# Attention's v turns in one copy and one difference each, filling products over both sequence halves of one w_o tile, the second w_o tile split behind them

## The chip, the cores and the metric

The kernel runs on one core of a Trainium2 chip. Its time is the time on the device of one execution, in microseconds (us); the median of several runs counts. The profile comes from one more execution, recorded by the hardware profiler. Engines are named as in the profile: PE multiplies matrices, PEld loads its weights, DVE works on vectors, ACT computes functions and copies, POOL is a third engine for elementwise work, and SP issues the transfers (DMAs). Each engine works through its own queue in order and waits there for the others by semaphores.

## The reference

Two layers of a decoder work on a sequence of 1024 positions of width 1024, in 32-bit floats. Layer 0 mixes with a linear recurrence, layer 1 with stick-breaking attention of 16 heads of 64 columns; a SwiGLU network follows each. What matters here is the attention:

```
qkv = einsum("bsd,de->bse", x, w_qkv)            # x: normalized input of the layer
for each block of 128 queries, keys s < t only:
    z        = q @ k.T / sqrt(64)
    log_fail = log_sigmoid(-z)                   # 0 where s >= t
    suffix   = reverse_cumsum(log_fail) - log_fail
    weights  = exp(log_sigmoid(z) + suffix)      # 0 where s >= t
    out      = weights @ v
o = concatenate(outs)                            # all heads side by side
return einsum("bse,ed->bsd", o, w_o)             # then h = h + this
```

## The kernel before

**Numbers in two parts.** Each 32-bit operand of a matrix product is split into a rounded high part and a low remainder. A product is then three matmuls, high by high, high by low, low by high (`mm3`, L141 to L143). A split is a copy on ACT (the high part) and a difference on DVE (the low part).

**Layout.** Activations lie transposed: 8 tiles of 128 columns of the model by 1024 positions, in two halves `n` of 512 positions. `xh[k][n]` and `xl[k][n]` are the parts of column tile k, half n. They hold the attention's input first, and take its result afterwards. In the profile they are called vh, vl and xg, after the memory that they share.

**The attention** goes through 8 pairs `q` of heads. A generator `fill` (`all_fill`) gives the projections of q, k and v for the next pair (`qkv_steps`), one `mm3` at a time, to be put between the steps of the present pair, which leave PE waiting otherwise. The loop at the end of `trunk` runs over units `u`, each a block of 128 keys against 512 queries. In one step of it stand, in this order: the scores of a later chunk (`z_part`, two matmuls into z_ps), the transposes of the weights of unit u + 2 (`t_part`, into wt_ps) and their split (`t_split`: ACT copy th at L1474, DVE difference tl at L1475), the rest of the chunk (`z_rest`), one deferred task from the list `later`, two steps of `fill`, and the products of unit u with v (`av_part`, L1486 and L1487, into av_ps).

`z_rest` makes two sigmoids on ACT (L1445, L1446), a scan on DVE from the right end of the chunk (L1449, L1451) and a product on POOL (L1452). F has one column more than the chunk, for what stands to its right. In chunks on the diagonal POOL sets it to 0 (L1438); for the four off-diagonal chunks of a head it is copied from `sofar[j]`, one column of 128, by ACT (L1441). POOL writes `sofar[j]` (L1454).

**A turn of v.** v must lie with the positions on the partitions, so each half of each pair's v is transposed in four blocks into a PSUM bank (`v_turn`, L1401). The bank holds 4 blocks by 2 heads by 64 columns. For each head in turn, ACT copies its 256 columns to the high part (L1405) and DVE forms the low part (L1406). The turns use the two buffers of the projections, but for the last one (pair 7, half 1), which borrows one of the two buffers of the weights' transposes, with tag "T".

**The end of the attention.** When all projections are done, `all_fill` goes on with products of the output projection: it splits the second tile of w_o (`mix[0].proc(1)`, ACT L168 and DVE L169), takes a PSUM tile `ob` with two halves, and multiplies, for the first two tiles of w_o in the order 0, 4, 1, 5, ..., half 0 of the column tiles k = 0 to 6, one `mm3` in every other step. Column tile 7 is missing, since the last pair of heads still computes it. Results of earlier pairs went to DRAM and are brought back by `bring_back` (L1315, L1316), both halves in one go.

Column tile 7 of half n is ready once `gather` (ACT L1496, DVE L1497) has put the two heads together and `parts` (ACT L1502, DVE L1503) has split them; for half 1 these are the last works of the attention.

`mix_out_ffn_in` follows. For its first four outputs it goes through (d, n) = (0, 0), (4, 0), (0, 1), (4, 1): the first two finish the halves of `ob` with column tile 7 of half 0, the third and fourth start in fresh banks (`dense_in`, 24 matmuls each, ob_ps).

The order on each engine is written out by hand in these places (`manual_schedule`). Where two such blocks meet, the instructions of both mix, each block's own order kept: so the six matmuls that finish the halves of `ob` stand among the attention's last products.

Of the kernel before, what the change touches and what calls it, by code (L numbers as in the profile page):

```python
# [16 lines left out]
P = 128  # L17
S = 1024
D = 1024
ND = D // P  # L20
NT = S // P
NB = 512
NH = S // NB
# [3 lines left out]
HD = 64  # L27
# [6 lines left out]
def trunk(  # L34
# [22 lines left out]
    nc = tc.nc  # L57
    f32 = lambda t: t.bitcast(F32)
# [40 lines left out]
    xh, xl = [None] * ND, [None] * ND  # L99
# [40 lines left out]
    def mm3(ps, wh, wl, mh, ml, first, last, **kw):  # L140
        nc.tensor.matmul(ps, lhsT=wh, rhs=mh, start=first, stop=False, **kw)  # L141
        nc.tensor.matmul(ps, lhsT=wh, rhs=ml, start=False, stop=False, **kw)  # L142
        nc.tensor.matmul(ps, lhsT=wl, rhs=mh, start=False, stop=last, **kw)  # L143
# [98 lines left out]
    half = lambda t, n: t[:, n * NB : (n + 1) * NB]  # L242
# [119 lines left out]
    with ExitStack() as st:  # L362
# [152 lines left out]
        with tc.manual_schedule(engines={E.PE}):  # L515
            for what in "A0 A1 B0 A2 G0 A3 Y0 B1 Y1 A4 G1 A5 B2 Y2 A6 G2 A7 B3 Y3 B4 Y4 G3 B5 Y5 B6 Y6".split():
                {"A": stage_a, "B": stage_b, "G": stage_g, "Y": stage_y}[what[0]](int(what[1]))
            mix = last_tile(ND - 1)
# [78 lines left out]
    def mix_out_ffn_in(h, mix, bias, layer, gnext, ob):  # L597
# [3 lines left out]
        half = lambda t, i: t[:, i * NB : (i + 1) * NB]  # L601
# [8 lines left out]
        begun = ob is not None  # L610
        if begun:
            ps_.enter_context(pos)
        else:
            po = ps_.enter_context(tc.tile_pool(name="fpo", bufs=1, space=PSUM, reuse_waits="tile"))
            ob = po.tile([P, S], F32, name="ob")
# [106 lines left out]
        with tc.manual_schedule(engines={E.PE, E.Activation, E.DVE, E.Pool}):  # L722
# [11 lines left out]
            w = None  # L734
            for j in range(HK):
                rows = (j, j + HK)
                dn = [(d, n) for d in rows for n in range(NH)] if j else [(d, n) for n in range(NH) for d in rows]
                for k, (d, n) in enumerate(dn):
                    o = HK * j + k
                    if begun and o < 2:  # L740
                        ps = half(ob, o)
                        for i in range(2 if o == 0 else 0):
                            hi, lo = mix.w[rows[i]]
                            mm3(half(ob, i), hi[:, ND - 1], lo[:, ND - 1], xh[ND - 1][0], xl[ND - 1][0], False, True)
                    else:
                        ps = pp.tile([P, NB], F32, tag="p", name="ob_ps")
                        dense_in(ps, mix.w[d], n)
                    if bias is None:
                        V.tensor_add(h[d][n], ps, h[d][n])
                    else:  # L750
                        V.scalar_tensor_tensor(
                            h[d][n], ps, vc[:, bias + d : bias + d + 1], h[d][n], op0=ALU.add, op1=ALU.add
                        )
                    for i in loads.get(o, ()):
                        mix.load(i)
                    if o in procs:
                        mix.proc(procs[o])
                    if o == 10:
                        w = weights_in(0)
                    elif o == 11:  # L760
                        w.s12()
                        w.s2()
                        w.s3()
                        w.do_s4()
                    elif o == 12:
                        w.a_hi()
                        w.a_lo()
                    elif o == 14:
                        w.b_hi()
                        w.b_lo()  # L770
                        nw = weights_in(1)
                    if o < 15:
                        drain(2)
                    if sq_todo:
                        squares(h, *sq_todo.pop(0), rbc[1:], acc)
                if j == HK - 1:
                    xstk.close()
                    open_v(xstk, v, False)
                    rhs_in = {i: [v[i, j] for j in range(HK)] for i in range(NPROD)}
                todo.append(v_steps(h, v, j, gcol, ta, tb))  # L780
                sq_todo += [(d, n) for d in rows for n in range(NH)]
# [291 lines left out]
            for s_, (kind, x) in enumerate(steps):  # L1073
                w, nw, ahead = nw, nxt, None
# [218 lines left out]
    with ExitStack() as st:  # L1293
        ap = st.enter_context(tc.tile_pool(name="ap", bufs=1))
        qs, mix = ExitStack(), [Mix(w_o, 0)]
# [9 lines left out]
        Q, KK, VV = {}, {}, {}  # L1305
# [65 lines left out]
        def evacuate(q, which, n, ps):  # L1371
            full = lambda tag, m: [ap.tile([P, m, S], F32R, tag=tag, name=tag, bufs=4) for _ in range(2)]
            t = ap.tile([P, NB], F32, tag="t", name="t", bufs=2)
            nc.vector.tensor_mul(t, ps, rbc[n])
            yield
            cs = slice(n * NB, (n + 1) * NB)
            if which == 0 and n == 0:
                Q[q] = [t[:, 0] for t in full("q", 1)]
            if which == 1 and n == 0:
                KK[q] = full("kk", 2)  # L1380
            if which < 2:
                two = ap.tile([P, 2, NB], F32R, tag="two", name="two", bufs=2)
                nc.scalar.copy(two[:, 0], t)
                nc.vector.tensor_sub(two[:, 1], t, f32(two)[:, 0])
                for hx, (a, b) in enumerate(((top, bot), (bot, top))):
                    if which == 0:
                        nc.sync.dma_start(f32(Q[q][hx])[a, cs], f32(two)[a, 0])
                        nc.sync.dma_start(f32(Q[q][hx])[b, cs], f32(two)[a, 1])
                    else:
                        for half_ in (top, bot):  # L1390
                            nc.sync.dma_start(f32(KK[q][hx])[half_, :, cs], f32(two)[a])
                return
            if n == 0:
                VV[q] = ap.tile([P, NT, 2, P], F32R, tag="v", name="v", bufs=2)

            def v_turn():

                pool, tag = (psT, "T") if (q, n) == (NP - 1, 1) else (psQ, "qk")
                tp = pool.tile([P, NB], F32, tag=tag, name="vt_ps")
                for i in range(4):  # L1400
                    nc.tensor.transpose(tp[:, i * P : (i + 1) * P], t[:, i * P : (i + 1) * P], ident)  # L1401
                src = tp.rearrange("p (b h c) -> p b h c", b=4, h=2)
                bs = slice(4 * n, 4 * n + 4)
                for hx in range(2):
                    nc.scalar.copy(VV[q][:, bs, hx, 0:HD], src[:, :, hx])  # L1405
                    nc.vector.tensor_sub(VV[q][:, bs, hx, HD:P], src[:, :, hx], f32(VV[q])[:, bs, hx, 0:HD])  # L1406

            late.append(v_turn)
            if q == NP - 1 and n == 0:
                bring_back(*((p, 0) for p in range(NP - 2)))  # L1410
# [22 lines left out]
        def z_rest(ps, q, hx, j, ci, c0, c1, diag):  # L1433
            n = min(c1, (j + 1) * P) - c0
            F = ap.tile([P, NB + 32], F32, tag="F", name="F", bufs=4)
            first = 0.0
            if diag:
                nc.gpsimd.memset(F[:, n : n + 1], 0.0)  # L1438
            else:
                first = sofar[j]  # L1440
                nc.scalar.copy(F[:, n : n + 1], first)  # L1441
            tag = f"w{j}" if diag else "w"
            wt = ap.tile([P, n], F32, tag=tag, name=tag, bufs=1 if diag else 4)
            W[q, hx, j, ci] = wt
            nc.scalar.activation(F[:, 0:n], ps[:, 0:n], AF.Sigmoid, scale=-SC)  # L1445
            nc.scalar.activation(wt, ps[:, 0:n], AF.Sigmoid, scale=SC)  # L1446
            rev = F[:, 0:n][:, ::-1]
            if diag:
                nc.vector.tensor_tensor_scan(rev, rev, unit[:, NB - n :][:, ::-1], first, op0=ALU.mult, op1=ALU.add)  # L1449
            else:  # L1450
                nc.vector.tensor_tensor_scan(rev, rev, rev, first, op0=ALU.mult, op1=ALU.bypass)  # L1451
            nc.gpsimd.tensor_mul(wt, wt, F[:, 1 : n + 1])  # L1452
            if diag and j >= 4:
                nc.gpsimd.tensor_copy(sofar[j], F[:, 0:1])  # L1454
# [65 lines left out]
        def all_fill():  # L1520
            yield from first
            for q in range(1, NP):
                yield from qkv_steps(q)
            bring_back((NP - 2, 0), *((p, 1) for p in range(NP - 2)))
            yield
            yield
            late.pop()()
            qs.close()
            mix[0].proc(1)
            po = pos.enter_context(tc.tile_pool(name="fpo", bufs=1, space=PSUM, side="right", reuse_waits="tile"))  # L1530
            ob = po.tile([P, S], F32, name="ob")
            mix.append(ob)
            for i, d in enumerate(mix[0].order[:2]):
                w = mix[0].w[d]
                for k in range(ND - 1):
                    mm3(ob[:, i * NB : (i + 1) * NB], w[0][:, k], w[1][:, k], xh[k][0], xl[k][0], k == 0, False)
                    yield
                    yield

        fill = all_fill()  # L1540
        ready = {}
        E = mybir.EngineType
        with tc.manual_schedule(engines={E.PE, E.Activation, E.DVE, E.Pool, E.SP}):
# [3 lines left out]
            first = qkv_steps(0)  # L1547
# [16 lines left out]
            c = 0  # L1564
# [69 lines left out]
```

## Time and profile before

| | us |
|---|---|
| median of 3 runs | 2195.4 |
| lowest and highest run | 2195.05, 2197.01 |
| the profiled execution, its own time | 2195.37 |
| its span, from the first to the last instruction | 2193.6 |
| granted TensorE clock, mean over the span | 0.998 |

Rows of the profile read like this. In the busy times by stretch stand the stretch, its length, then for PE, PEld, DVE, ACT and POOL the busy time and the number of instructions, then the granted clock of TensorE (1.00 is full speed), the share of the DMA engines and GB/s. In groups of instructions stand line, engine, operation, output and inputs with their shapes and count, then busy time in us and the mean of one in ns, then the idle time of the engine before them and what ended it. In the order of time stand the start and the duration in us, and in brackets the idle time just before and who ended it. Waits have the engine and line that waited, who ended it, us in total, the number of times and the longest. In rows of one line of the code stand the least, the median and the greatest duration in ns. The duration of a matmul holds its way through the array: matmuls of 512 columns follow each other every 0.23 us, though each is shown with 0.39. Lines are those of the kernel before; in the changed kernel the attention's lines stand two later.

### The profile page before, as it was taken

The numbers are of one execution on the slowest core, as the hardware profiler recorded it, in microseconds if no ns is written. First come the engines' busy times: TensorE is split into PE (matmuls) and PEld (weight loads), VectorE is DVE, ScalarE is ACT, GpSimd is POOL, SyncE is SP. The second block draws the span as 40 slices with busy tenths as digits, with TensorE's granted clock in tenths as the row PEclk, the third lists the DMA queues.
The fourth block names the chain that finished last, engine by engine and source line by source line (L and its number), as shares of the span: only waits on it lengthen the run. The fifth ranks groups of instructions, "written<-read, shape, count | busy, mean of one in ns | idle before, by whom it ended". The sixth has DMA issues, their size and how long they took to land.

```text
span 2193.6 us, 28494 instructions
## 1 busy us (share of the span) xinstructions
PE 2167.9 (99%) x10120; PEld 1803.3 (82%) x10120; DVE 1711.4 (78%) x2383; ACT 1155.4 (53%) x2031; POOL 315.7 (14%) x443
## 2 busy tenths in 40 slices
PE   8999999999999999999999999999999999999998
PEld 6888888888888888888888888878888888888887
DVE  6887778667777887887888888876876777788886
ACT  5567435334444544556666666753543444454556
POOL 2222020000000000004444444531000000000002
PEclk9999999999999999999999999999999999999999
DMA  7111412334444764434333333551133444467442
GB/s 232 49 48 39 135 39 64 110 125 152 141 145 138 250 221 129 148 117 104 89 106 90 94 98 105 173 169 54 48 115 116 149 146 143 144 228 236 137 153 87
DMA packets 297677, 277.71 MB, mean 127 GB/s; under 512 B 15288, under 2 KB 214080, under 8 KB 297536
## 3 DMA queue, kind: packets, MB, share of 16 engines
q1 hardware_dynamic: 297520, 275.90, 40.6%
q8 instruction: 79, 1.29, 0.2%
q14 instruction: 62, 0.51, 0.1%
q10 hardware_dynamic: 16, 0.00, 0.0%
HBM read 175.71 MB, written 74.97 MB: 114 GB/s over the span
## 4 chain that ended last, share of the span: by engine, by line
PE 95%; DVE 2%; ACT 1%; DMA 1%; SPq 0%; issue 0%; DVEq 0%; ACTq 0%
PE p_ps L143 18%; PE p_ps L141 18%; PE p_ps L142 18%; PE qk_ps L143 4%; PE qk_ps L141 4%; PE qk_ps L142 4%; PE wt_ps L1465 3%; PE ob_ps L141 2%; PE ob_ps L142 2%; PE ob_ps L143 2%; PE a_ps L141 2%; PE a_ps L142 2%; PE a_ps L143 2%; PE z_ps L1427 2%; PE z_ps L1428 2%; PE av_ps L1487 2%
## 5 line engine op out<-in xcount | busy, mean ns | idle before, releaser
L1452 POOL TENSOR_TENSOR w<-w,F 128x128 f32<-128x128 f32 (+1 forms) x192 | 192.5, 1002 | 268.3 <-DVE F L1449 164.6
L141 PE MATMUL p_ps<-vh,wch 128*128 128x512 f32 x524 | 204.2, 390 | 0.0
L143 PE MATMUL p_ps<-vh,wal 128*128 128x512 f32 x524 | 204.1, 389 | 0.1
L143 PE MATMUL p_ps<-vh,wbl 128*128 128x512 f32 x524 | 204.1, 390 | 0.0
L143 PE MATMUL p_ps<-vh,wcl 128*128 128x512 f32 x524 | 204.1, 390 | 0.0
L141 PE MATMUL p_ps<-vh,wbh 128*128 128x512 f32 x524 | 204.1, 390 | 0.0
L142 PE MATMUL p_ps<-vl,wch 128*128 128x512 f32 x524 | 203.9, 389 | 0.0
L142 PE MATMUL p_ps<-vl,wbh 128*128 128x512 f32 x524 | 203.9, 389 | 0.0
L141 PE MATMUL p_ps<-vh,wah 128*128 128x512 f32 x524 | 203.9, 389 | 0.0
L142 PE MATMUL p_ps<-vl,wah 128*128 128x512 f32 x524 | 203.8, 389 | 0.0
L668 ACT CAST wbh<-sb 128x1024 fp32r<-128x1024 f32 (+2 forms) x69 | 69.6, 1009 | 193.1 <-DVE sb L652 193.1
L1474 ACT CAST th<-wt_ps 128x512 fp32r<-128x512 f32 x192 | 92.6, 482 | 126.3 <-PE wt_ps L1465 125.8
L212 POOL TENSOR_TENSOR acc<-acc,rbc 128x512 f32<-128x512 f32 x30 | 41.6, 1386 | 771.9 <-ACT rbc L211 771.9
L1475 DVE TENSOR_TENSOR tl<-wt_ps,th 128x512 fp32r<-128x512 f32 x192 | 105.6, 550 | 48.9 <-ACT th L1474 46.9
L141 PE MATMUL qk_ps<-vh,whi 128*128 128x512 f32 x264 | 118.1, 447 | 0.0
L1449 DVE TENSOR_TENSOR_SCAN F<-F,unit 128x128 f32<-128x128 f32 (+3 forms) x128 | 115.4, 902 | 2.8 <-ACT F L1445 2.6
L143 PEld LDWEIGHTS p_ps<-vh,wbl 128*128 128x128 f32 x524 | 98.4, 188 | 21.4 <-DVE wbl L672 0.8
L143 PEld LDWEIGHTS p_ps<-vh,wal 128*128 128x128 f32 x524 | 98.3, 188 | 21.4 <-DVE wal L663 1.0
L143 PEld LDWEIGHTS p_ps<-vh,wcl 128*128 128x128 f32 x524 | 98.3, 188 | 21.1 <-DVE wcl L682 0.6
L141 PEld LDWEIGHTS p_ps<-vh,wch 128*128 128x128 f32 x524 | 98.4, 188 | 20.8 <-ACT tb L1057 0.5
L141 PEld LDWEIGHTS p_ps<-vh,wah 128*128 128x128 f32 x524 | 98.4, 188 | 20.4
L142 PEld LDWEIGHTS p_ps<-vl,wah 128*128 128x128 f32 x524 | 98.4, 188 | 20.4
(341 smaller groups left out, 5858.3 us busy)
## 6 DMA issues: line engine op xcount, KB each, us to landing
raw<-in_ffn_w_in SPq DMA_DIRECT2D x88, 512.0 KB, 4.0
vl<-pd SPq DMA_DIRECT2D x128, 256.0 KB, 3.6
pd<-U SPq DMA_DIRECT2D x90, 256.0 KB, 2.3
kk<-two SPq DMA_DIRECT2D x64, 256.0 KB, 4.2
raw<-in_ffn_w_out SPq DMA_DIRECT2D x56, 256.0 KB, 3.9
raw<-in_attn_w_qkv SPq DMA_DIRECT2D x24, 512.0 KB, 4.1
raw<-in_lru_w_in SPq DMA_DIRECT2D x16, 512.0 KB, 4.0
q<-two SPq DMA_DIRECT2D x64, 128.0 KB, 2.3
```

Of the source, the lines that this page charges most:

```text
L141: nc.tensor.matmul(ps, lhsT=wh, rhs=mh, start=first, stop=False, **kw)
L142: nc.tensor.matmul(ps, lhsT=wh, rhs=ml, start=False, stop=False, **kw)
L143: nc.tensor.matmul(ps, lhsT=wl, rhs=mh, start=False, stop=last, **kw)
L668: nc.scalar.copy(self.full(self.wb), self.full(self.sb))
L1427: nc.tensor.matmul(ps[:, 0 : c1 - c0], lhsT=lhsT, rhs=KK[q][hx][:, 0, c0:c1], start=True, stop=False)
L1428: nc.tensor.matmul(ps[:, 0 : c1 - c0], lhsT=lhsT, rhs=KK[q][hx][:, 1, c0:c1], start=False, stop=True)
L1449: nc.vector.tensor_tensor_scan(rev, rev, unit[:, NB - n :][:, ::-1], first, op0=ALU.mult, op1=ALU.add)
L1452: nc.gpsimd.tensor_mul(wt, wt, F[:, 1 : n + 1])
L1465: nc.tensor.transpose(tp[:, c : c + P], W[q, hx, j, kb // 4][:, (kb % 4) * P : (kb % 4 + 1) * P], ident)
L1474: nc.scalar.copy(th[:, q0:], tp[:, q0:])
L1475: nc.vector.tensor_sub(tl[:, q0:], tp[:, q0:], f32(th)[:, q0:])
L1487: nc.tensor.matmul(ps[:, q0:], lhsT=VV[q][:, kb, hx], rhs=tl[:, q0:], start=False, stop=last)
```

## The change

- In `v_turn` the two copies become one over both heads, and the two differences one.
- In `z_rest` the one-column copy of `sofar[j]` into F goes from ACT to POOL.
- In `all_fill` the fourteen filling products take one tile of w_o, d = 0, with both halves, in place of tiles 0 and 4 with half 0. The split of the second w_o tile stands behind these products in place of ahead of them.
- In `mix_out_ffn_in` the first four outputs of the second layer are now (0, 0), (0, 1), (4, 0), (4, 1). Both halves of `ob` are finished at the start with column tile 7, each with its own half of it.

```diff
@@ mix_out_ffn_in
-                dn = [(d, n) for d in rows for n in range(NH)] if j else [(d, n) for n in range(NH) for d in rows]
+                dn = [(d, n) for d in rows for n in range(NH)]
+                if j == 0 and not begun:
+                    dn = [(d, n) for n in range(NH) for d in rows]
                 for k, (d, n) in enumerate(dn):
                     o = HK * j + k
                     if begun and o < 2:
                         ps = half(ob, o)
+                        hi, lo = mix.w[d]
                         for i in range(2 if o == 0 else 0):
-                            hi, lo = mix.w[rows[i]]
-                            mm3(half(ob, i), hi[:, ND - 1], lo[:, ND - 1], xh[ND - 1][0], xl[ND - 1][0], False, True)
+                            mm3(half(ob, i), hi[:, ND - 1], lo[:, ND - 1], xh[ND - 1][i], xl[ND - 1][i], False, True)
@@ v_turn
-                for hx in range(2):
-                    nc.scalar.copy(VV[q][:, bs, hx, 0:HD], src[:, :, hx])
-                    nc.vector.tensor_sub(VV[q][:, bs, hx, HD:P], src[:, :, hx], f32(VV[q])[:, bs, hx, 0:HD])
+                vh, vl = (VV[q][:, bs, :, c] for c in (slice(0, HD), slice(HD, P)))
+                nc.scalar.copy(vh, src)
+                nc.vector.tensor_sub(vl, src, f32(vh))
@@ z_rest
-                nc.scalar.copy(F[:, n : n + 1], first)
+                nc.gpsimd.tensor_copy(F[:, n : n + 1], first)
@@ all_fill
-            mix[0].proc(1)
             po = pos.enter_context(tc.tile_pool(name="fpo", bufs=1, space=PSUM, side="right", reuse_waits="tile"))
             ob = po.tile([P, S], F32, name="ob")
             mix.append(ob)
-            for i, d in enumerate(mix[0].order[:2]):
-                w = mix[0].w[d]
+            w = mix[0].w[mix[0].order[0]]
+            for n in range(NH):
                 for k in range(ND - 1):
-                    mm3(ob[:, i * NB : (i + 1) * NB], w[0][:, k], w[1][:, k], xh[k][0], xl[k][0], k == 0, False)
+                    mm3(half(ob, n), w[0][:, k], w[1][:, k], xh[k][n], xl[k][n], k == 0, False)
                     yield
                     yield
+            mix[0].proc(1)
```

## The prediction

> **What bounds the kernel now.** I read the page first, then busy time by stretch, PE's waits, and the order of time around each wait.
>
> ```profile
> PE 2167.9 (99%) x10120; PEld 1803.3 (82%) x10120; DVE 1711.4 (78%) x2383; ACT 1155.4 (53%) x2031; POOL 315.7 (14%) x443
> ```
> ```profile
> 980.00:1422.00 442.00, 440.94 (x2355) 373.28 (x2355) 374.20 (x540) 294.72 (x726) 194.57 (x354) 1.00 0.40 106
> 1422.00:1436.00 14.00, 10.30 (x51) 8.44 (x51) 12.98 (x17) 9.04 (x24) 6.79 (x8) 0.88 0.86 292
> 1436.00:1452.00 16.00, 16.00 (x90) 13.51 (x89) 14.61 (x21) 12.53 (x32) 11.21 (x21) 1.00 0.31 101
> 1452.00:1466.00 14.00, 11.53 (x62) 9.74 (x61) 10.31 (x15) 7.41 (x16) 3.17 (x3) 0.88 0.00 0
> 1466.00:1556.00 90.00, 90.00 (x399) 74.53 (x398) 61.05 (x77) 37.41 (x59) 13.37 (x10) 1.00 0.29 91
> ```
> ```profile
> PE wt_ps L1465 <- DVE v L1406: 2.5, 1, 2.5
> PE wt_ps L1465 <- DVE tl L1475: 2.5, 2, 1.4
> PE vt_ps L1401 <- DVE tl L1475: 1.2, 1, 1.2
> ```
>
> PE is the bound: 440.94 of 442 us busy in the attention's main stretch, and in all of attention it waits for another engine four times, 6.2 us in all (the last fence, read with a window on attention). All four lie at attention's end, where the projections that fill PE have run out. After it PE has no gap in 90 us. So what the change does to ACT, DVE and POOL counts only where it moves PE between 1422 and 1470 us.
>
> **The change part by part.** *Turns of v.* Sixteen turns lose one ACT and one DVE instruction each, and the alternation between the two engines. What two halves cost now, and what one DVE difference of 512 columns costs, these groups show:
>
> ```profile
> L1405 ACT CAST v<-vt_ps 128x256 fp32r<-128x256 f32 x32 | 12.0, 374 | 21.9 <-DVE v L1406 17.7 <-PE vt_ps L1401 4.0
> ```
> ```profile
> L1475 DVE TENSOR_TENSOR tl<-wt_ps,th 128x512 fp32r<-128x512 f32 x96 | 65.9, 687 | 41.2 <-ACT th L1474 40.1
> L1406 DVE TENSOR_TENSOR v<-vt_ps,v 128x256 fp32r<-128x256 f32 x32 | 13.5, 421 | 8.7 <-ACT v L1405 8.5
> ```
>
> On DVE 2 x 0.421 becomes about 0.69, and ACT's 17.7 us of waiting for DVE between its copies goes. Fifteen turns cost or give nothing: PE's 440.94 us cover them. The sixteenth, head pair 7's second half, borrows a PSUM buffer of the transposes of w, and PE waits for it:
>
> ```profile
> 1428.61 0.69 DVE L1497 TENSOR_TENSOR oo<-av_ps,oo 64x512 f32<-64x512 f32 x1
> 1429.34 0.42 DVE L1406 TENSOR_TENSOR v<-vt_ps,v 128x256 fp32r<-128x256 f32 x1
> 1430.20 0.42 DVE L1406 TENSOR_TENSOR v<-vt_ps,v 128x256 fp32r<-128x256 f32 x1 [0.44 <-ACT v L1405]
> 1431.15 1.23 DVE L169 TENSOR_TENSOR wlo<-raw,whi 128x1024 fp32r<-128x1024 f32 x1 [0.52 <-ACT whi L168]
> ```
> ```profile
> 1430.77 1.08 PE L1465 MATMUL wt_ps<-ident,w 128*128 128x128 f32 x4 [2.55 <-DVE v L1406]
> ...
> 1433.75 0.49 PE L1465 MATMUL wt_ps<-ident,w 128*128 128x128 f32 x3
> ...
> 1438.57 0.60 PE L1465 MATMUL wt_ps<-ident,w 128*128 128x128 f32 x4
> ...
> 1440.17 0.60 PE L1465 MATMUL wt_ps<-ident,w 128*128 128x128 f32 x4
> ```
>
> The differences take 1429.34 to 1430.62, 1.28 us. One of 0.69 in their place frees the buffer 0.59 us sooner: **-0.6**, bounds 0 and -2.55 (the whole wait). DVE's work ahead of it (scans, gather) stays, so some 1.95 us of waiting stay.
>
> *The clock behind that wait.* Windows of 3.41 us, laid where the clock steps, show what the wait costs besides:
>
> ```profile
> 1426.87:1430.28 3.41, 1.35 (x8) 1.01 (x6) 2.91 (x4) 0.48 (x2) 1.72 (x2) 1.00 0.88 283
> 1430.28:1433.69 3.41, 2.92 (x11) 2.65 (x12) 2.89 (x5) 3.41 (x9) 0.00 (x0) 0.50 0.81 297
> 1454.17:1457.59 3.42, 1.26 (x9) 1.08 (x10) 3.29 (x5) 0.72 (x3) 2.10 (x2) 1.00 0.00 0
> 1457.59:1461.00 3.41, 3.41 (x16) 3.11 (x15) 2.50 (x5) 2.36 (x5) 0.09 (x1) 0.50 0.00 0
> ...
> 10.33:13.75 3.42, 1.53 (x10) 1.13 (x10) 3.42 (x6) 3.04 (x5) 1.82 (x1) 1.00 1.14 321
> 13.75:17.16 3.41, 2.81 (x12) 2.34 (x13) 1.47 (x3) 3.37 (x6) 2.71 (x2) 1.00 0.44 134
> ```
>
> After a window with PE busy 1.35 or 1.26 us, the next runs at clock 0.50; after one with 1.53 it does not. Here that costs about 1.4 us: one step of four transposes, three products and four small matmuls took 1430.77 to 1433.75, 2.98 us, and the same step at full clock 1438.57 to 1440.17, 1.60. With 1.95 us of waiting left, at least 3.41 - 1.95 = 1.46 us are busy in any such window, between 1.35 and 1.53: undecided. Bounds -1.4 (the slow window goes) and +0.3 (it stays, and half of the 0.6 is lost in it); I take **-0.4**, nearer to its staying.
>
> *The second w_o tile.* Its ACT copy and DVE difference leave 1430 to 1432, where no PE wait names them, for a place behind the last scan, in front of the second difference of the last head:
>
> ```profile
> 1457.93 0.42 DVE L1475 TENSOR_TENSOR tl<-wt_ps,th 128x256 fp32r<-128x256 f32 x1 [0.47 <-ACT th L1474]
> ```
> ```profile
> 1457.05 0.44 PE L1465 MATMUL wt_ps<-ident,w 128*128 128x128 f32 x2 [1.42 <-DVE tl L1475]
> ...
> 1461.89 0.40 PE L141 MATMUL ob<-vh,whi 128*128 128x512 f32 x1
> ...
> 1464.70 0.39 PE L142 MATMUL ob<-vl,whi 128*128 128x512 f32 x1
> 1464.93 0.39 PE L143 MATMUL ob<-vh,wlo 128*128 128x512 f32 x1
> 1465.15 0.40 PE L1487 MATMUL av_ps<-tl,v 128*128 128x512 f32 x1
> 1465.39 0.39 PE L141 MATMUL ob_ps<-vh,whi 128*128 128x512 f32 x1
> ```
>
> DVE's 1.23 us are now in the chain transpose, copy, difference, product. But DVE idles 0.47 us right there, and PE itself runs at half clock until 1461.00. Following the chain with these durations, the last product of attention comes 0.15 us later for it (bounds 0 and +1.23). Three matmuls (those at 1461.89, 1464.70, 1464.93) no longer stand ahead of it: 0.35 us earlier (bounds 0 and 3 x 0.23 = 0.69). Together **-0.2**.
>
> *Both halves of one tile.* The fourteen products keep their places and number, only their operands change. The last product of each half needs head pair 7's outcome. Before, both were of half 0, long done, and half 1's stood 21 matmuls further on. Now half 1's stands right behind attention's last product at 1465.15, and waits for all of this:
>
> ```profile
> 1465.59 0.58 ACT L1496 COPY oo<-av_ps 64x512 f32<-64x512 f32 x1 [1.34 <-PE av_ps L1487]
> 1466.92 0.62 ACT L1502 CAST vh<-oo 128x512 fp32r<-128x512 f32 x1 [0.76 <-DVE oo L1497]
> ```
> ```profile
> 1467.58 0.69 DVE L1503 TENSOR_TENSOR vl<-oo,vh 128x512 fp32r<-128x512 f32 x1 [0.69 <-ACT vh L1502]
> ```
>
> The first matmul waits for vh, done at 1467.54; the second for vl, done at 1468.27. Two more steps of 0.23 us, and the work that began at 1465.39 begins near 1468.81: **+3.4** (bounds +2.4, if only vh held it, and +3.9, with half a microsecond of further hand-over). Behind it in PE's queue stands all of the rest, so this is paid in full. The halves that come back from DRAM are no new wait: the last is issued at 1433.78 and lands in about 5.7 us, the first of half 1 is used near 1440.5, and it was issued first, at 1427.05:
>
> ```profile
> 1427.05 0.32 SPq L1315 DMA_DIRECT2D vh<-odh  x1
> ...
> 1433.78 0.32 SPq L1316 DMA_DIRECT2D xg<-odl  x1
> ```
>
> *The clock behind the new wait.* Its two idle parts are 2.0 and 0.35 us, so a window of 3.41 us can have as little as 1.0 us of PE work, under 1.35, but only in about half of its possible positions; then the next 3.4 us lose 1.7. Bounds 0 and +1.7; **+0.8**.
>
> Here a rule speaks against the measured price: the Trainium skill, "TensorE: Matmul & The Clock Gate", section "Part 1: The HAM clock gate (the "warmup" mystery)", has the PE fall back to half rate after at least one idle window of some 3.4 us. The rows above disagree, since windows with 1.26 and 1.35 us of work were enough. By the rule neither wait would slow anything, and the sum would be 1.2.
>
> *The one-column copy* goes from ACT to POOL, 64 times:
>
> ```profile
> L1441 ACT COPY F<-sofar x64: 194/195/231, 1006.5 to 1452.7; 128x1 f32<-128x1 f32 x64
> ```
> ```profile
> L1454 POOL COPY sofar<-F x64: 176/184/1122, 999.9 to 1448.2; 128x1 f32<-128x1 f32 x64
> ```
>
> The like POOL copy takes 0.18 us, at most 1.12, when it sits until a DVE scan has ended. In POOL's queue only the product that needs that same scan is behind it, and transposes read that product several steps later. Nothing, bounds 0 and +0.6 (three copies among the final scans at 0.2). The four first outputs come in another order, at equal work under PE's full 90 us: 0.
>
> Sum against the profiled execution's 2195.37 us: -0.6 - 0.4 - 0.2 + 3.4 + 0.8 = +3.0, **2198.4 us**. That execution lies 0.03 under the median of the runs, so nothing is corrected.
>
> **Rivals.** *Slower by over 0.2% (4.4 us; less than that a measurement of this kernel hardly tells from no change).* The clock halves behind the new wait, and still behind the old one: -0.3 - 0.2 + 3.4 + 1.7 = +4.6, 2200.0; with the moved split fully on the chain 2201.1. It decides where the window around 1466 holds under about 1.4 us of PE work. For it: 1.0 is possible. Against: the position of the windows. Chance 0.23.
>
> *The clock never halves at either wait.* -0.6 - 1.4 - 0.2 + 3.4 = +1.2, 2196.6. For it: 1.46 against 1.53 at the first wait, and the windows' position at the second. Chance 0.15.
>
> *Faster.* DVE's relief near 1431 (0.59 + 0.52 + 1.23) reaches the two waits for tl at 1454 and 1457, 2.5 us together: -0.6 - 1.4 - 2.5 - 0.2 + 3.4 = -1.3, 2194.1; below 2191 only if something also covered the new wait. Against it: between, PE is full for 16 us and DVE waits for it again. Chance 0.06, of which 0.03 under 2191.
>
> *No effect* would need half 1's last product to find its operand ready; nothing between 1465.59 and 1468.27 can be skipped.
>
> **How the numbers follow.** The forecast has 0.56, 2196.6 to 2199.8. With the neighbours the range is 2195.6 to 2200.8. Faster by over 0.2%: 0.03; slower: the rival's 0.23; within: the rest, 0.74.
>
> **What would show it.** PE's waits should hold a new one of about 2 us on ACT's vh and a short one on DVE's vl behind attention's last product; the wait on v near 2.0 instead of 2.55; the main stretch unchanged; clock 0.50 in the window behind the new wait, or not. I am wrong if the new wait is missing, if waits appear before 1422 us, or if the waits at 1454 to 1457 change by over a microsecond.

## The result and the profile after

| | before | changed |
|---|---|---|
| median, us | 2195.16 (9 runs) | 2202.16 (9 runs) |
| lowest and highest run | 2194.81, 2197.01 | 2198.94, 2203.71 |
| ratio of the times, 95% interval | | 1.0027 [1.0018, 1.0035] |
| profiled execution | 2195.37 | 2200.38 |
| its span | 2193.6 | 2198.6 |
| PE busy in it | 2167.9 | 2169.4 |

The changed kernel is slower by 7.0 us in the median and by 5.0 in the profiled execution. Forecast were 2198.4 and a range up to 2200.8, so the time lies 1.4 us beyond the range. Of the profiled execution's 5.0 us PE is busy for 1.5 and idle for 3.5.

Busy time by stretch of the changed kernel (PE, PEld, DVE, ACT, POOL, then the granted clock):

```profile
980.00:1422.00 442.00, 440.98 (x2357) 373.31 (x2355) 371.57 (x525) 289.05 (x654) 222.16 (x410) 1.00 0.40 106
1422.00:1436.00 14.00, 10.93 (x61) 8.86 (x60) 13.94 (x18) 9.93 (x25) 10.11 (x15) 1.00 0.97 337
1452.00:1466.00 14.00, 8.98 (x44) 7.03 (x43) 10.56 (x16) 6.58 (x12) 3.45 (x4) 0.88 0.18 57
1466.00:1476.00 10.00, 8.79 (x31) 6.92 (x32) 4.01 (x6) 2.61 (x3) 0.00 (x0) 0.83 1.01 347
1476.00:1556.00 80.00, 80.00 (x355) 66.24 (x354) 53.12 (x66) 30.16 (x47) 13.35 (x10) 1.00 0.20 59
```

The main stretch is as it was: PE 440.98 of 442 us (440.94 before), with ACT's time down and POOL's up by the copies that moved. From 1476 on PE is full again. All that changed lies between 1422 and 1476. There PE's waits are now these (a window on attention, as in the prediction):

```profile
PE wt_ps L1467 <- DVE tl L1477: 3.8, 3, 1.4
PE ob L141 <- ACT vh L1504: 2.0, 1, 2.0
PE wt_ps L1467 <- DVE v L1408: 2.0, 1, 2.0
PE vt_ps L1403 <- DVE tl L1477: 1.1, 1, 1.1
...
PE ob L142 <- DVE vl L1505: 0.2, 1, 0.2
PE av_ps L1489 <- DVE tl L1477: 0.2, 1, 0.2
```

The wait on v fell from 2.5 to 2.0, and the new waits on vh (2.0) and vl (0.2) are there. But the waits for tl rose from 2.5 us, 2 times, to 3.8, 3 times. The third one is new. In the order of time PE shows it, and what follows, in the changed kernel:

```profile
1430.24 0.63 PE L1467 MATMUL wt_ps<-ident,w 128*128 128x128 f32 x4 [1.97 <-DVE v L1408]
...
1431.88 0.49 PE L1467 MATMUL wt_ps<-ident,w 128*128 128x128 f32 x3
...
1455.20 0.44 PE L1467 MATMUL wt_ps<-ident,w 128*128 128x128 f32 x2 [1.43 <-DVE tl L1477]
...
1457.43 0.47 PE L1467 MATMUL wt_ps<-ident,w 128*128 128x128 f32 x1 [1.32 <-DVE tl L1477]
...
1464.45 0.49 PE L1489 MATMUL av_ps<-tl,v 128*128 128x512 f32 x1 [0.17 <-DVE tl L1477]
1466.99 0.50 PE L141 MATMUL ob<-vh,whi 128*128 128x512 f32 x1 [2.04 <-ACT vh L1504]
1467.71 0.79 PE L142 MATMUL ob<-vl,whi 128*128 128x512 f32 x1 [0.22 <-DVE vl L1505]
1468.30 0.63 PE L143 MATMUL ob<-vh,wlo 128*128 128x512 f32 x1
1468.73 0.63 PE L141 MATMUL ob_ps<-vh,whi 128*128 128x512 f32 x1
...
1471.17 0.39 PE L141 MATMUL ob_ps<-vh,whi 128*128 128x512 f32 x1
```

and in the kernel before, the two rows that the prediction did not quote:

```profile
1457.97 0.41 PE L1465 MATMUL wt_ps<-ident,w 128*128 128x128 f32 x1
...
1466.75 0.39 PE L141 MATMUL ob_ps<-vh,whi 128*128 128x512 f32 x1
```

Read as start after minus start before, for the same instruction, these rows follow the time along PE's queue:

| instruction | before | changed | difference |
|---|---|---|---|
| transposes that waited for v | 1430.77 | 1430.24 | -0.53 |
| the two transposes behind the last scan | 1457.05 | 1455.20 | -1.85 |
| the single transpose after them | 1457.97 | 1457.43 | -0.54 |
| last product of attention | 1465.15 | 1464.45 | -0.70 |
| first product in a fresh bank | 1465.39 | 1468.73 | +3.34 |
| the seventh of these | 1466.75 | 1471.17 | +4.42 |

The difference of -1.85 comes from the wait on v (-0.53) and from the half clock behind it, which this execution did not have. Then 1.31 us are lost again in one step, at the single transpose. The new wait takes 4.04 to the first fresh product and the clock behind it another 1.08. The last 0.6 us to the end of the span come in small pieces.

### The profile page after: what moved, and what is told of

Its sections match the earlier page's. It is cut to its first block, busy times and chain, and to the rows that moved or that the text cites. A ratio compares the mean times of both kernels' runs of the same rounds, so it can differ in the third digit from the quotient of the medians.

```text
span 2198.6 us, 28406 instructions
## 1 busy us (share of the span) xinstructions
PE 2169.4 (99%) x10120; PEld 1803.0 (82%) x10120; DVE 1709.9 (78%) x2367; ACT 1149.2 (52%) x1951; POOL 345.8 (16%) x507
## 4 chain that ended last, share of the span: by engine, by line
PE 94%; DVE 3%; ACT 1%; DMA 1%; SPq 0%; issue 0%; DVEq 0%; ACTq 0%
PE p_ps L143 18%; PE p_ps L141 18%; PE p_ps L142 18%; PE qk_ps L143 4%; PE qk_ps L141 4%; PE qk_ps L142 4%; PE wt_ps L1467 3%; PE ob_ps L142 2%; PE ob_ps L141 2%; PE ob_ps L143 2%; PE a_ps L141 2%; PE a_ps L143 2%; PE a_ps L142 2%; PE z_ps L1429 2%; PE z_ps L1430 2%; PE av_ps L1489 2%
## 5 line engine op out<-in xcount | busy, mean ns | idle before, releaser
L141 PEld LDWEIGHTS p_ps<-vh,wbh 128*128 128x128 f32 x524 | 98.4, 188 | 20.5 <-ACT ta L1059 0.2
```

## The experiments

All times are medians in us of 7 to 11 runs, beside 27 to 30 runs of the kernel before on the same chip. The last column is the mean of the runs' granted clock, with that of the kernel before beside it. A window of 3.41 us at half clock lowers a run's mean clock by 3.41 x 0.5 / 2198.6 = 0.0008 and costs up to 1.7 us. The column can't be turned into time, though. Besides those at attention's end the profiles have such windows between 10 and 19 us, where PE waits for its first operands (two in e2's, none in the first of the changed kernel, and yet e2 comes to attention's first scores at 989.81 us, the changed kernel at 990.49), and the clock halves once more behind PE's last product of all.

| experiment | median | minus before | ratio, 95% interval | clock (before) |
|---|---|---|---|---|
| e1_changed_again | 2202.04 | +6.40 | 1.003 [1.002, 1.0041] | 0.9961 (0.9979) |
| e2_half1_later | 2197.91 | +2.27 | 1.0014 [1.0005, 1.0023] | 0.9967 (0.9979) |
| e3_split_ahead | 2198.81 | +3.17 | 1.0016 [1.0007, 1.0025] | 0.9975 (0.9979) |
| e4_turn_and_copy | 2194.49 | -1.15 | 0.9995 [0.9986, 1.0003] | 0.9987 (0.9979) |
| e5_mid | 2196.26 | +0.15 | 1.0 [0.9991, 1.0009] | 0.9981 (0.9978) |
| e6_later_and_ahead | 2195.84 | -0.27 | 0.9996 [0.9987, 1.0005] | 0.9983 (0.9978) |
| e7_split_on_pool | 2195.42 | -0.69 | 0.9997 [0.9988, 1.0006] | 0.9983 (0.9978) |
| e8_wait_kept_warm | 2201.27 | +5.16 | 1.0024 [1.0014, 1.0035] | 0.9966 (0.9978) |
| e9_turn_alone | 2195.20 | -0.48 | 0.9994 [0.9985, 1.0003] | 0.9983 (0.9980) |
| e10_copy_alone | 2195.74 | +0.06 | 1.0001 [0.9992, 1.001] | 0.9974 (0.9980) |
| e11_changed_split_on_pool | 2198.39 | +2.71 | 1.0013 [1.0004, 1.0022] | 0.9974 (0.9980) |

Each interval is about 2 us wide to either side, so a single difference of one microsecond between two experiments says little. What follows rests on differences of 2.5 us and more, each found in at least two pairs, and on rows.

**The changed kernel once more**, unchanged, as the point that the others are compared with.

> The changed kernel, unchanged. Its nine runs so far had a median 7.0 us over the kernel before, its profile only 5.0, and the mean granted clock of the runs lies between 0.995 and 0.998 (0.998 in the profile). Theory A: the 2 us that the profile lacks are windows of half clock (each lowers the mean by 0.0008 and costs up to 1.7 us), set off by the new waits at the end of attention; then another profile shows, depending on where the windows of 3.4 us fall, up to three more windows at 0.50 between 1426 and 1475 us, and time and mean clock of the runs go together. Rival B: the 2 us lie elsewhere (steps of attention stretched by the POOL copies, or the second network); then the windows at half clock are the same two as in the first profile while the time is 2 us longer.

It came out at +6.40. Its profiled execution (2201.5 us) has the same waits, but for 3.0 us in place of 3.8 in the three for tl, and besides a half-clock window behind the wait on v that the first profile of the changed kernel lacks. Windows of 3.41 us, laid within 0.1 us of where the clock steps:

```profile
1427.60:1431.01 3.41, 1.43 (x11) 1.17 (x10) 3.35 (x5) 1.68 (x4) 2.62 (x4) 1.00 0.96 304
1431.01:1434.42 3.41, 3.41 (x15) 3.03 (x13) 2.66 (x4) 1.22 (x4) 1.85 (x4) 0.51 1.01 352
...
1468.55:1471.96 3.41, 3.18 (x8) 2.48 (x8) 2.27 (x4) 1.99 (x2) 0.00 (x0) 0.51 1.04 317
```

With one more near 1458.4, as in the first profile, three half-clock windows stand behind waits of the same kind here and two there, and the execution with less waiting is the longer one: from the transposes of the last turn of v to attention's last product it takes 40.74 us (1424.82 to 1465.56), the first one 39.99 (1424.46 to 1464.45).

**Without the new wait.** Half 1's last product of ob goes behind the 24 matmuls of output (4, 0); the second w_o tile stays behind the fill.

```diff
-                if j == 0 and not begun:
+                if j == 0:
                     dn = [(d, n) for n in range(NH) for d in rows]
...
-                    if begun and o < 2:
-                        ps = half(ob, o)
+                    if begun and o in (0, 2):
+                        ps = half(ob, n)
                         hi, lo = mix.w[d]
-                        for i in range(2 if o == 0 else 0):
-                            mm3(half(ob, i), hi[:, ND - 1], lo[:, ND - 1], xh[ND - 1][i], xl[ND - 1][i], False, True)
+                        mm3(ps, hi[:, ND - 1], lo[:, ND - 1], xh[ND - 1][n], xl[ND - 1][n], False, True)
```

> As changed, but the last product of ob's half 1 (column tile 7) stands behind the 24 matmuls of output (4, 0), so that it finds its operand ready; everything else of the change stays. Theory A (the new wait on vh and vl, and the half clock that it sets off, carry the loss): the 2.0 and 0.2 us of waiting go and the window at half clock behind them too; 2193.5 to 2195.5, 0.9995 of the kernel before, and the runs lie close together again. Rival B (the loss beyond the profile's 4.4 us at that place comes from elsewhere): 2196.5 to 2198.

**With the new wait, split ahead.** `mix[0].proc(1)` goes back ahead of the filling products, all else as changed.

```diff
+            mix[0].proc(1)
             po = pos.enter_context(tc.tile_pool(name="fpo", bufs=1, space=PSUM, side="right", reuse_waits="tile"))
...
-            mix[0].proc(1)
```

> As changed, but the second w_o tile is split ahead of the filling products, as before the change. Theory A: the wait of 1.3 us for tl at 1457 us goes, and DVE's 1.23 us return to 1431 us, where no PE wait names them: 1 to 2 us faster than the changed kernel, 2200 to 2201. Rival (as in the prediction, the moved split costs 0.15): no difference, 2202. If the split at the old place lengthens the wait for the turn of v, PE's wait on v at 1430 us is over 2.0.

**Only the turn of v and the copy on POOL**, on the kernel before (the `v_turn` and `z_rest` parts of the change).

> The kernel before with the turn of v in one copy and one difference and the one-column copy on POOL, nothing else. Theory A: PE's wait on v falls from 2.55 to 2.0 us, the window at half clock behind it goes in some runs: 2193 to 2194.8, 0.4 to 2.0 faster than before. Rival B (the POOL copies stretch DVE's scans or the steps of attention): 2196 or more, and attention's main stretch is longer than before.

These three with the first make a table of two by two, all with the new turn and copy:

| | no wait on vh, vl | wait on vh, vl |
|---|---|---|
| split ahead of the fill | -1.15 (e4) | +3.17 (e3) |
| split behind the fill | +2.27 (e2) | +6.40 (e1) |

The new wait costs 4.3 in the first row and 4.1 in the second, the moved split 3.4 in the first column and 3.2 in the second. The runs of e2 and e4 don't overlap at all (2196.31 and up, 2195.90 and down), those of e1 and e3 hardly (2200.34 and up, 2201.17 and down). But e4 has besides the filling products and the first outputs of the kernel before. e6 below differs from e2 in the place of the split alone, and stands at -0.27: with it in e4's place the wait costs 3.4 and 4.1, the split 2.5 and 3.2. Within the intervals the two add. The wait had been forecast at 3.4 + 0.8, the place of the split at +0.15. e4 came out as its first theory expected, e2 as its rival did, and e3 faster than both of its theories. In e2, with no wait on vh, PE waits instead 0.5 us for a result further on, hh, and its waits for tl are those of the changed kernel:

```profile
PE wt_ps L1466 <- DVE tl L1476: 3.7, 3, 1.4
...
PE ob L141 <- DVE hh L750: 0.5, 1, 0.5
```

and two windows follow each other at half clock (laid within 0.1 us of its steps):

```profile
1451.80:1455.20 3.40, 1.36 (x9) 1.05 (x9) 3.40 (x5) 1.54 (x3) 3.19 (x3) 1.00 0.00 0
1455.20:1458.61 3.41, 2.15 (x10) 1.73 (x9) 2.98 (x6) 1.68 (x4) 0.00 (x0) 0.51 0.29 89
1458.61:1462.02 3.41, 3.41 (x15) 3.01 (x15) 1.94 (x3) 1.17 (x2) 0.00 (x0) 0.50 0.45 142
```

What the moved split costs thus arises without the new wait; the wait for tl that grew lies at 1455 to 1457 in the changed kernel, ten microseconds ahead of that one. In e3, which has the wait but not the moved split, the waits for tl are back near the old sum:

```profile
PE wt_ps L1467 <- DVE tl L1477: 2.9, 4, 1.4
PE ob L141 <- ACT vh L1504: 2.0, 1, 2.0
```

**What in the moved split costs.** A split is an ACT copy and a DVE difference. Here is what DVE and POOL do in the changed kernel where the moved split now stands:

```profile
1454.49 0.66 DVE L1477 TENSOR_TENSOR tl<-wt_ps,th 128x512 fp32r<-128x512 f32 x1
1455.07 1.83 DVE L169 TENSOR_TENSOR wlo<-raw,whi 128x1024 fp32r<-128x1024 f32 x1
1456.83 0.87 DVE L1477 TENSOR_TENSOR tl<-wt_ps,th 128x384 fp32r<-128x384 f32 x2
...
1468.77 1.23 DVE L169 TENSOR_TENSOR wlo<-raw,whi 128x1024 fp32r<-128x1024 f32 x1 [1.11 <-ACT whi L168]
```
```profile
1454.74 1.09 POOL L1454 TENSOR_TENSOR w<-w,F 128x512 f32<-128x512 f32 x1 [0.19 <-DVE F L1453]
```

The difference wlo takes 1.83 us (1.46 in e1, 1.84 in e2) and not the 1.23 of the next tile's, and the 384-wide tl, which PE's single transpose waits for, stands behind it. POOL's product, 1454.74 to 1455.83, lies beside it. If DVE stands still until that has ended, 1455.83 - 1455.07 = 0.76 us are waiting and 1.07 are work. The same sum gives 0.76 + 1.08 in e2 and 0.39 + 1.07 in e1, where the product ended 0.39 us behind the start of wlo. The Trainium skill, "SBUF — State Buffer", section "Who interferes with whom", has such a rule: a DVE instruction with two inputs in SBUF and a GpSimd instruction that reads SBUF exclude each other, and the later one stands still until the earlier has ended. The trace agrees with it here, with 1.83 against 1.23 and the same 1.07 or 1.08 of work in all three. How much of the loss is this standing still and how much the mere place in the queue, no run separates.

So the difference was taken off DVE, in e2's kernel and then in the changed one:

```diff
-        def proc(self, i):
+        def proc(self, i, eng=None):
...
-            nc.vector.tensor_sub(lo, raw, f32(hi))
+            (eng or nc.vector).tensor_sub(lo, raw, f32(hi))
...
-            mix[0].proc(1)
+            mix[0].proc(1, nc.gpsimd)
```

> As e2_half1_later (no wait on vh and vl, split behind the fill), but the difference of the second w_o tile (128x1024) runs on POOL behind POOL's last product, not on VectorE. Theory A (VectorE's 1.83 us ahead of the 384-wide tl is what makes PE wait 1.3 us there and lets a further half-clock window come): the 384-wide tl comes 1 to 1.8 us sooner, the wait of PE at it falls from 1.26 to about 0.2, and the time is 2194.5 to 2195.5. Rival (the lost time comes from what the scalar copy of the tile or the missing fill does, not from VectorE's difference): 2197 to 2198. A middle outcome, 2195.5 to 2197: POOL's difference takes so long (2 us or more) that output (4,0) waits for wlo, or slows the tl beside it.

> The changed kernel, wait on vh and vl included, with the difference of the second w_o tile on POOL, not on VectorE. Theory (the place in VectorE's order is all that the moved split costs, and it adds to the wait): 2.5 to 3.5 us below the changed kernel, 2198.3 to 2199.5 where the kernel before has 2195.2 to 2196.1, the wait of PE at the one-transpose tl gone and the scatter of its runs no more than 3 us. Rival (with the wait on vh and vl still there, PE loses there what it gains here, or the half-clock windows come anyway): 2200.5 to 2202.5, with runs 4 us or more apart.

The first fell from +2.27 to -0.69, the second from +6.40 to +2.71: 3.0 and 3.7 us, as much as the moved split costs. ACT's copy of the tile stayed where it was in both, so it isn't the cause. In e7 POOL takes the work behind its last product, and the wait at the single transpose is gone:

```profile
1454.05 1.09 POOL L1453 TENSOR_TENSOR w<-w,F 128x512 f32<-128x512 f32 x1 [0.19 <-DVE F L1452]
1455.09 2.38 POOL L169 TENSOR_TENSOR wlo<-raw,whi 128x1024 fp32r<-128x1024 f32 x1
```
```profile
PE wt_ps L1466 <- DVE tl L1476: 2.5, 2, 1.4
```

One half of e11's expectation failed: its runs lie between 2195.98 and 2201.98, 6 us apart, where at most 3 had been expected. Behind the wait on vh and vl a half-clock window stands in some executions (the profiles of the changed kernel, e1 and e11) and not in others (e3's). Its profiled execution (2200.48) is one of the slower ones, and shows POOL's difference in the way of DVE in its turn:

```profile
1457.93 2.37 POOL L169 TENSOR_TENSOR wlo<-raw,whi 128x1024 fp32r<-128x1024 f32 x1
```
```profile
1459.29 1.56 DVE L1505 TENSOR_TENSOR vl<-oo,vh 128x512 fp32r<-128x512 f32 x1 [0.36 <-ACT vh L1504]
```

The vl of half 0 takes 1.56 us, and 0.69 in all other executions; PE waited 0.8 for it.

**The split in the middle, and ahead.** Both keep half 1's last product late (e2's edit). In e5 the split stands between the seven products of half 0 and those of half 1 (`if n == 0: mix[0].proc(1)` inside the loop over n); in e6 ahead of all fourteen.

> Half 1's last product of ob behind the 24 matmuls of output (4,0), as in e2_half1_later, and the second w_o tile split between the 7 filling products of half 0 and the 7 of half 1 rather than behind all 14. Theory A (the place of the split in VectorE's order is what costs 3 us: behind all fills its difference runs beside POOL's last product for 1.8 us instead of 1.2 and stands ahead of the 384-wide tl): with the split earlier than that and no wait on vh and vl, about the level of e4_turn_and_copy, 2193.5 to 2195.5, with one half-clock window in the diagonal part. Rival (any split behind the start of the fill pushes the chain of tl): 2196.5 to 2198, as e2_half1_later.

> Half 1's last product behind output (4,0) and the second w_o tile split ahead of the fill, as the kernel before does: what is left of the change is the turn of v, the POOL copy and which seven products fill. Theory A (split 3.2 to 3.4, wait on vh and vl 4.3, the two add): 2194 to 2195, as e4_turn_and_copy, since the 14 products fill the same places. Rival (the products of half 1 need something of the second sequence half that is late, or half 1's later last product leaves a wait of its own, such as the 0.5 us on hh of e2_half1_later): 2195 to 2196.5.

Both are at the level of the kernel before, +0.15 and -0.27, with 2.8 and 2.7 us of waits for tl in place of e2's 3.7. So it isn't a split inside the fill that costs, but one on DVE behind the last scan. In absolute time both came 0.8 us above the first theory's range, where the kernel before too had 0.5 more than beside e4; e6 lies in the range of its rival, which named the 0.5 us that PE waits on hh in both; e5 lies between its two ranges. Against e4's -1.15 they lose some of the turn's gain, by less than the intervals can tell.

**The wait, filled.** In the changed kernel eleven matmuls, whose results are not used, stand between half 0's and half 1's last products, so that PE works while vh and vl come.

```diff
                         for i in range(2 if o == 0 else 0):
+                            if i:
+                                warm = pp.tile([P, NB], F32, tag="p", name="warm_ps")
+                                for r in range(11):
+                                    nc.tensor.matmul(warm, lhsT=hi[:, 0], rhs=xh[0][0], start=True, stop=True)
```

> The changed kernel with 11 matmuls of 512 columns (results unused, an own bank) between half 0's and half 1's last product of ob, so that PE works through the time in which vh and vl come; all else as changed. At the 0.22 us of a full-clock matmul these take 2.4 us, at half clock up to 4.7. Theory A (of the 4.3 us that the new order costs, 2.3 to 3.3 are the waiting and 0.8 to 1.7 the half clock that it sets off): the half-clock window at 1467 to 1471 goes, the wait on vh falls to nothing, and the time is 0.5 to 1.7 us below the changed kernel's, 2200.3 to 2201.5. Rival (the half clock behind the wait is set off by the waits on tl ten us before, not by this one): the window stays, the added matmuls run at half clock, and the time is 0 to 2 us above the changed kernel's.

```profile
1465.66 2.68 PE L749 MATMUL warm_ps<-vh,whi 128*128 128x512 f32 x11
...
1469.16 0.40 PE L141 MATMUL ob_ps<-vh,whi 128*128 128x512 f32 x1
1469.40 0.39 PE L142 MATMUL ob_ps<-vl,whi 128*128 128x512 f32 x1
```

The half clock behind the wait is gone: the products follow each other every 0.23 us, where the changed kernel has 0.43. The time is +5.16 against +6.40, inside what the first theory expected, though the intervals of the two overlap. The runs still spread over 5.4 us, and the profile still has two half-clock windows in a row at 1457 to 1463. e2, which has the moved split and no new wait, has two in a row at the same place. From attention's last product to the 21st in fresh banks e8 takes 8.40 us, the changed kernel 9.92.

**The two small parts alone**, on the kernel before.

> The kernel before with one edit of the change: a turn of v leaves its bank in one copy and one difference. Theory (the prediction's first two terms): the wait on v falls from about 2.6 to 2.0 us and its half-clock window shrinks or goes, 0.6 to 1.4 us below the kernel before, and this edit alone is the gain of e4_turn_and_copy (1.15). Rival (the gain of e4 comes from the POOL copy, which takes a copy of one column off ScalarE ahead of the scans): the wait on v still falls to 2.0, but the time is within 0.4 us of the kernel before.

> The kernel before with one edit of the change: the one-column copy into F on POOL, not on ScalarE. Theory (the prediction's term of 0): within 0.4 us of the kernel before, the waits of PE in the diagonal part as before. Rival (the POOL copy, which sits 1.1 us beside a scan, slows VectorE or POOL's products, or frees ScalarE): 0.5 us or more off the kernel before, in either direction.

The copy gives +0.06, nothing, as forecast. The turn gives -0.48, short of the 0.6 expected of it, and together with the copy -1.15 (e4). With intervals of 2 us these can't be told apart, nor from no gain. The runs of e9 fall into two heaps, which suggest why: five from 2192.76 to 2194.16 with clocks of 0.998 to 1.000, and six from 2195.20 to 2196.92 with 0.996 to 0.998. The wait on v is 1.9 or 2.0 us in all profiles with the new turn, and 2.6 in e10 with the old one; whether a half-clock window follows it changes from profile to profile.

None of these kernels is faster than the kernel before by more than its interval.

## Why the prediction failed

**The second w_o tile: forecast +0.15 for the new place of its split, measured +2.5 to +3.7 (e2 less e6, e7 and e4; e1 less e3 and e11). This is the step that failed.** It said that of DVE's 1.23 us only 0.15 would reach the last product, since "DVE idles 0.47 us right there, and PE itself runs at half clock". Three things were wrong.

- The idle 0.47 lies behind the differences that the moved one was put in front of. Up to there DVE has no idle time. The kernel before, in a window of 4 us that ends where they begin (DVE is the third busy time):

```profile
1452.00:1456.00 4.00, 2.58 (x18) 2.07 (x16) 4.00 (x5) 2.81 (x7) 2.08 (x2) 1.00 0.00 0
```

  Even with the prediction's own 1.23 us the 384-wide tl, done at 1456.34 + 1.12 = 1457.46 before, would have ended at 1458.69, and the single transpose that waits for it began at 1457.97: 0.72 us late, in a stretch in which PE has no further gap. If half of that is won back while PE runs at half clock, some 0.36 us are left (an estimate), and not 0.15.

- The duration was 1.83 and not 1.23. The row of 1.23 was taken from a place where POOL was idle; at the new place POOL's last product runs. PE waits 1.32 us for the next tl (0.94 in e1), about the upper bound of 1.23 that the prediction gave to this step, and not the 0.15 that it took.
- It had no term for the clock. PE's waits of 1.05, 1.43 and 1.32 us now come within five and a half microseconds, and the runs with the split behind the fill on DVE have the lowest mean clocks of all (0.9961, 0.9967, 0.9966 in e1, e2, e8, against 0.9974 to 0.9987 in the others). In the profiles, the way from the transposes of the last turn of v to attention's last product takes 39.99, 40.74, 40.91 and 41.20 us with the split there (changed, e1, e2, e8), with one, two, two and two half-clock windows in it; it takes 38.34, 38.81, 39.49, 38.54 and 40.00 us in e3, e5, e6, e7 and e11, with none in e3 and one in each of the others. That is 1.7 us more in the mean, and nearly one window more. Of the 2.5 to 3.7 us of the medians PE's wait for the next tl is 0.9 to 1.3; that the rest is half clock fits this, but how many windows a median execution has was not seen, and so its size stays open.

The prediction had written beside it that it would be wrong if the waits at 1454 to 1457 changed by over a microsecond. They did, from 2.5 to 3.8. The other part of the term, three matmuls that no longer stand ahead (-0.35), shows as -0.16 from the single transpose to attention's last product, with a new wait of 0.17 us for tl in it.

**The turn of v, -0.6:** right. The wait fell from 2.55 to 1.97 us.

**The clock behind it, -0.4 of -1.4 to +0.3:** left open, and rightly. A half-clock window follows the wait in five of the eleven profiles with the new turn. With the windows counted back from the clock's steps, the one that holds most of the wait has 1.43 or 1.44 us of PE work in these five and 1.63 to 2.39 in the other six, so where the windows lie decides, as the prediction had it with its 1.46. The turn gave -0.5, turn and copy -1.15, against a forecast of -1.0 for both terms.

**The new wait, +3.4, and the clock behind it, +0.8:** right. PE waits 2.04 us for vh and 0.22 for vl; in the medians the pair of terms, 4.2 forecast, is 4.3 (e3 less e4) and 4.1 (e1 less e2), and 3.4 in e3 less e6 and in e11 less e7. The rows tell the two terms apart: from attention's last product to the 21st in fresh banks the kernel before takes 4.77 us, e3, with no half clock there, 8.38, and the changed kernel, e1 and e11, with a window, 9.92, 9.92 and 10.00. So the wait costs 3.6 and the window 1.5 or 1.6 more, in single executions. (The prediction's own steps, 1468.27 + 2 x 0.23, end at 1468.73 and not at 1468.81; that would be +3.3.)

**The one-column copy and the order of the first outputs, 0 each:** right. e10 has +0.06, and PE is busy for 80.00 of 80 us behind 1476.

**The rivals.** What happened is nearest to the slower one, 2200.0 to 2201.1, chance 0.23, but it looked for the extra half clock behind the two known waits, and had none for the moved split. The faster one, DVE's relief at 1431 reaching the waits at 1454 and 1457, did not come: the waits of 1.05 and 1.43 us stand in the changed kernel too. Against the Trainium skill's rule of one idle window ("TensorE: Matmul & The Clock Gate", section "Part 1: The HAM clock gate (the "warmup" mystery)") the runs agree with the rows of before: windows with 0.9 to 1.7 us of work were followed by half clock.

With the difference of the second w_o tile off DVE, e11 stands at +2.7 where the sum said +3.0, so the rest of the sum holds within e11's interval (+0.9 to +4.8). With +2.5 to +3.7 in place of +0.15 the sum would be +5.4 to +6.6, where +6.4 and +7.0 were measured: this one term makes the error.

## What to carry to other kernels

Before a piece of work is moved in an engine's queue, read at the new place what stands right behind it and who waits for that, and take its duration from a row with the same neighbours on the other engines, not from a quiet place. A small delay on a queue that is already late can cost more than its length when the matrix engine's clock halves behind idle time; price that for every wait that grows, not only for the ones that are new. And if two edits are in one change, a table of two by two of the four kernels tells which one costs.

## What the runs showed of the hardware

DVE and POOL hold each other up in both directions, and which one loses varies. In e10 DVE's last scan ran in 1.26 us and POOL's product beside it took 2.69; in e7 the scan took 1.64 and the product beside it 1.09. The rows of e10:

```profile
1454.45 2.69 POOL L1452 TENSOR_TENSOR w<-w,F 128x512 f32<-128x512 f32 x1 [0.19 <-ACT th L1474]
```
```profile
1454.98 1.26 DVE L1451 TENSOR_TENSOR_SCAN F<-F,sofar 128x512 f32<-128x512 f32 x1
```

and those of e7:

```profile
1451.71 1.09 POOL L1453 TENSOR_TENSOR w<-w,F 128x512 f32<-128x512 f32 x1 [0.19 <-ACT th L1475]
```
```profile
1452.24 1.64 DVE L1452 TENSOR_TENSOR_SCAN F<-F,sofar 128x512 f32<-128x512 f32 x1
```

In both the product starts 0.53 us ahead of the scan. In e7 it ends as if alone and the scan is longer, in e10 it is the other way round, so a start in the trace doesn't tell which of the two goes first.

PE's busy time in a window of 3.41 us doesn't decide alone whether the next one runs at half clock. The prediction had read a border between 1.35 and 1.53 us. With the windows counted back from the clock's step, e10 has one with 1.56 us that was followed by full clock and one with 1.69 that was followed by half:

```profile
1427.13:1430.54 3.41, 1.56 (x9) 1.22 (x8) 3.06 (x3) 0.26 (x1) 3.13 (x4) 1.00 0.92 305
1430.54:1433.96 3.42, 2.70 (x16) 2.32 (x17) 2.75 (x4) 3.42 (x10) 0.00 (x0) 1.00 1.03 328
1454.44:1457.85 3.41, 1.69 (x11) 1.41 (x12) 2.94 (x6) 0.96 (x4) 3.32 (x3) 1.00 0.01 2
1457.85:1461.26 3.41, 3.41 (x16) 3.07 (x15) 2.62 (x5) 2.32 (x5) 0.58 (x1) 0.50 0.00 0
```

At attention's end in the thirteen profiles, full-clock windows with 1.44 us and less were all followed by half clock and those with 1.77 and more by none; between these both occur. A window that was itself at half clock was followed by another where PE was busy for 2.15 (e2) and 2.51 us (e8) of it, and not with 2.91 (before) and more.

What the clock's control counts instead was not tried.
